# Substitution in 16x16 blocks by columns in place of rows, in a gated DeltaNet layer

## The chip, the cores and the metric

The kernel runs on one core of a Trainium2 chip. The metric is the device time of one execution in microseconds, of which the median of several runs is taken. The profile shows one further execution, instruction by instruction, on five engines: TensorE (PE; its weight loads are PEld), VectorE (DVE), ScalarE (ACT), GpSimd (POOL) and SyncE (SP), which issues most DMAs.

## What the reference computes

One layer of a hybrid backbone over 2048 latent tokens and 256 context tokens, 1024 wide: an adaLN-modulated input, a projection to 10272 columns, a bidirectional gated DeltaNet with 8 heads of 128 (branch A), a gated short convolution (branch B), a merge, an output projection and a LayerNorm. What the change touches is the inverse of a unit triangular matrix in each chunk of branch A:

```python
m = jnp.where(tri_strict, jnp.einsum('bhncd,bhnsd->bhncs', k_beta, k) * decay, 0.0)
eye = jnp.eye(CHUNK, dtype=jnp.float32)
t_inv = lax.linalg.triangular_solve(eye + m, jnp.broadcast_to(eye, m.shape), left_side=True, lower=True)
u = jnp.einsum('bhncs,bhnsv->bhncv', t_inv, v_beta)
...
v_new = u_i - jnp.einsum('bhck,bhkv->bhcv', w_i, s)
o = jnp.einsum('bhck,bhkv->bhcv', q_dec_i, s) + jnp.einsum('bhcs,bhsv->bhcv', qk_i, v_new)
s = s * d_i[..., None, None] + jnp.einsum('bhck,bhcv->bhkv', k_dec_i, v_new)
```

## The kernel before

The program has three parts. First come the projections (`projections`, `strassen`), which leave q, k, v, gates and decays in HBM. Then comes a window (`window`), in which 36 visits (18 chunks of 128 tokens in two directions, d = 0 and d = 1, in turn) carry the state, while the dense products of branch B and of the output of branch A ("fillers", L1249 to L1253) fill TensorE between the visits' own products. Last comes `final`, the output projection.

A visit inverts a 128x128 unit triangular matrix for each of 8 heads, by doubling: blocks of 16, then 32, 64 and 128. Its steps are spread over four turns of a loop, in which v0 to v3 are four successive visits. In one turn the loop writes, in this order: the state's product for v0 (`st_ks`, L300, and its sum on VectorE, L302), the loads of v3 (`visit_load`, among them gcb, the decays of all heads, L104), the first product of the 32-blocks for v1 (`inv_w16`, L210), the QK product for v2 (`gram`, L158, and its product with the decays on VectorE, L167, a piece for each head), the second one for v1 (`inv_d16`, L222, with L224 and L226 on VectorE, which write r32 and its transpose r32t), the decays of v3 (`visit_decay`, L128 to L142), the values, outputs and state sums of v0 (`st_v` L309, `st_o` L320 and L321, `st_u` L328 and L333 on VectorE) with the 64-blocks (`inv_w32`, L247, reads r32t) and 128-blocks (`inv_w64`, L278, reads r64t) of v1 between them, and at the end N for v3 (`gram`, L158 and L167) and its 16-blocks (`inv_base`). What `inv_base` makes for a visit is read one whole turn later, by `inv_w16`.

In 20 of the 36 visits, those of the four context chunks and the first to reach a latent chunk, N is formed in this way; 16 of them are latent and form QK so too. In the other 16 both come from HBM, kept by the visit in the other direction, and are multiplied by the decays in one piece each (L152).

TensorE runs in the order in which the loop is written. The instructions of every other engine are put in order by a planner when the program is built: among those whose inputs it takes to be ready it goes by the order in which they are written, and each engine then runs its list in that order.

`inv_base` takes the diagonal 32-blocks of -N by ACT (L177), folds the 16-blocks of each into 16 columns (n16: L180 on ACT, L181 and L182 on VectorE), and solves for R, the inverses of all 16x16 blocks, with 16 rows of each block in 16 partitions, and 8 heads of 16 columns in each partition. R begins as the identity (L185, GpSimd). The substitution goes row by row: row i of R is spread over the 16 partitions of its block (a shuffle, L191), multiplied by column i of n16 (L192) and added to R (L193). Each of the three reads what the one before has written. Then ACT spreads R into r32 (L196) and VectorE transposes it into r32t (L198).

Of the kernel before, what the change touches and what calls it, by code (L numbers as in the profile page):

```python
# [7 lines left out]
F32 = mybir.dt.float32  # L8
FR = mybir.dt.float32r
AF = mybir.ActivationFunctionType  # L10
ALU = mybir.AluOpType
# [4 lines left out]
P = 128  # L16
D = 1024
KT = 8
H = 8
# [13 lines left out]
def bc(ap, n):  # L33

    return ap.to_broadcast([ap.shape[0], ap.shape[1], n])


class Kern:
# [132 lines left out]
    def inv_base(self, v):  # L171
        nc, g2, d, N = self.nc, self.g2, v["d"], v["N"]

        v["n32"] = n32 = g2.tile([P, H, 32], F32, name="n32")
        for g in range(4):
            s = slice(32 * g, 32 * g + 32)
            nc.scalar.mul(out=n32[s], in_=N[s, :, s], mul=-1.0)  # L177
        n16 = g2.tile([P, H, 16], F32, name="n16")
        rows = lambda t: t.unsqueeze(1).to_broadcast([P, H, 16])
        nc.scalar.mul(out=n16, in_=n32[:, :, 0:16], mul=self.m16[0])  # L180
        nc.vector.scalar_tensor_tensor(out=n16, in0=n32[:, :, 16:32], scalar=self.m16[1], in1=n16, op0=ALU.mult, op1=ALU.add)  # L181
        nc.vector.tensor_tensor(out=n16, in0=n16, in1=rows(self.tri16[d]), op=ALU.mult)  # L182

        R = g2.tile([P, H, 16], F32, name="R16")
        nc.gpsimd.tensor_copy(out=R, in_=rows(self.i16))  # L185
        rb = g2.tile([P, H, 16], F32, name="rb")
        for i in (range(15, 0, -1) if d == 0 else range(0, 15)):
            c0, c1 = (i, 16) if d == 0 else (0, i + 1)
            w = c1 - c0
            rbv = rb.rearrange("p h c -> p (h c)")[:, 0:H * w].rearrange("p (h c) -> p h c", c=w)  # L190
            nc.vector.stream_shuffle(rbv, R[:, :, c0:c1], [i] * 16 + [16 + i] * 16)  # L191
            nc.vector.tensor_tensor(out=rbv, in0=rbv, in1=bc(n16[:, :, i:i + 1], w), op=ALU.mult)  # L192
            nc.vector.tensor_tensor(out=R[:, :, c0:c1], in0=R[:, :, c0:c1], in1=rbv, op=ALU.add)  # L193
        v["r32"] = r32 = g2.tile([P, H, 32], F32, name="r32")
        for hf in range(2):
            nc.scalar.mul(out=r32[:, :, 16 * hf:16 * hf + 16], in_=R, mul=self.m16[hf])  # L196
        v["r32t"] = r32t = g2.tile([P, H, 32], F32, name="r32t")
        nc.vector.transpose(self.fl(r32t), self.fl(r32))  # L198
# [1447 lines left out]
```

## Time and profile before

| what | value |
|---|---|
| median of 3 runs | 3217.88 us (3211.53 to 3222.15) |
| the profiled execution | 3213.67 us |
| its span, first to last instruction | 3211.9 us |
| PE busy | 2935.4 us (91%) |
| DVE busy | 2222.2 us (69%) |
| ACT busy | 1512.2 us (47%) |
| POOL busy | 1467.2 us (46%) |
| mean granted TensorE clock | 0.965 |

Busy time is the time in which an engine has at least one instruction in work; instructions of one engine may overlap at their ends. The shares are over the whole span, while the substitution runs from 1840 to 2836 us alone. The chain of waits goes back from the last instruction to what released it, step by step; what lies on it set the end.

### The profile page before, as it was taken

How to read it: one execution, taken by the hardware profiler on the slowest of the kernel's cores; microseconds unless marked ns; L12 is line 12 of the kernel's file. 1: busy time of each engine (PE TensorE's matmuls, PEld its weight loads, DVE VectorE, ACT ScalarE, POOL GpSimd, SP SyncE). 2: the span in 40 equal slices, each digit the busy share in tenths (PEclk: the TensorE clock that was granted, in tenths of full speed). 3: DMA queues.
4: the chain of work that ended last, by engine and by line, in shares of the span. 5: the costliest groups of instructions: out<-in, count | busy, mean ns of one | idle time of the engine just before them, and what ended most of it. 6: DMA issues, size and time to landing. Idle time of an engine off the chain costs nothing.

```text
span 3211.9 us, 60563 instructions
## 1 busy us (share of the span) xinstructions
PE 2935.4 (91%) x22089; PEld 2411.4 (75%) x22089; DVE 2222.2 (69%) x5843; ACT 1512.2 (47%) x3405; POOL 1467.2 (46%) x1080
## 2 busy tenths in 40 slices
PE   7899899999998999999999988898999889896997
PEld 4678668888887777788878767788887777784776
DVE  7756746566656575566652268999999988866399
ACT  4564554333445646333344335555656656652121
POOL 3543547766567555566656402333322132315264
PEclk9999999999999999999999989999999889998999
DMA  5533773323565433222233387667677777787742
GB/s 211 143 110 90 231 221 112 102 79 122 175 195 173 126 89 97 58 88 79 79 124 109 117 283 253 218 235 254 212 264 272 261 237 264 247 268 248 238 152 102
DMA packets 405384, 557.26 MB, mean 173 GB/s; under 512 B 28245, under 2 KB 278614, under 8 KB 404061
## 3 DMA queue, kind: packets, MB, share of 16 engines
q1 hardware_dynamic: 395982, 545.94, 52.6%
q10 hardware_dynamic: 9102, 7.45, 0.7%
q8 instruction: 173, 2.83, 0.4%
q14 instruction: 127, 1.03, 0.1%
HBM read 391.66 MB, written 161.64 MB: 172 GB/s over the span
## 4 chain that ended last, share of the span: by engine, by line
PE 47%; DVE 26%; issue 7%; DMA 6%; ACT 6%; POOL 4%; SPq 1%; DVEq 0%; ACTq 0%; POOLq 0%
PE pd L763 12%; PE pd L764 12%; PE pd L765 12%; DVE R L193 3%; DVE rb L192 3%; POOL al L347 2%; DVE gcb L140 2%; DVE rb L191 2%; DVE t L1008 1%; DMA gcb<-gcd 1%; POOL s L749 1%; PE pf L1253 1%; ACT n L177 1%; PE pf L1249 1%; DVE t L1010 1%
## 5 line engine op out<-in xcount | busy, mean ns | idle before, releaser
L763 PE MATMUL pd<-bh,ah 128*128 128x512 f32 x2240 | 890.5, 398 | 10.4 <-ACT u L783 5.8
L765 PE MATMUL pd<-bh,al 128*128 128x512 f32 x2240 | 877.7, 392 | 0.0
L764 PE MATMUL pd<-bl,ah 128*128 128x512 f32 x2240 | 877.0, 392 | 0.0
L347 POOL TENSOR_TENSOR al<-s,ah 128x512 fp32r<-128x512 f32 x348 | 478.9, 1380 | 471.9 <-ACT ah L346 459.9
L347 POOL TENSOR_TENSOR al<-raw,ah 128x512 fp32r<-128x512 f32 x260 | 372.0, 1435 | 321.7 <-ACT ah L346 296.0
L763 PEld LDWEIGHTS pd<-bh,ah 128*128 128x128 f32 x2240 | 423.9, 189 | 98.9 <-issue 6.6
L765 PEld LDWEIGHTS pd<-bh,al 128*128 128x128 f32 x2240 | 423.4, 189 | 90.7 <-POOL al L347 0.4
L764 PEld LDWEIGHTS pd<-bl,ah 128*128 128x128 f32 x2240 | 424.3, 189 | 85.4
L346 ACT CAST ah<-s 128x512 fp32r<-128x512 f32 x352 | 214.6, 618 | 299.7 <-PE pd L764 265.8
L346 ACT CAST ah<-raw 128x512 fp32r<-128x512 f32 x264 | 162.4, 616 | 263.5 <-PE pd L764 166.7
L749 DVE TENSOR_TENSOR s<-s,raw 128x512 f32<-128x512 f32 x80 | 107.1, 1338 | 220.5 <-POOL s L749 216.3
L1249 PE MATMUL pf<-ah,wh 128*128 128x512 f32 x512 | 213.0, 417 | 43.1 <-DMA wh<-w_ahd 20.9
L1253 PE MATMUL pf<-ah,wl 128*128 128x512 f32 x512 | 219.3, 429 | 5.1 <-DMA wl<-w_ald 5.1
L1251 PE MATMUL pf<-al,wh 128*128 128x512 f32 x512 | 213.1, 416 | 2.1 <-POOL al L347 1.3
L138 POOL TENSOR_TENSOR qd<-qd,qT 128x1024 f32<-128x1024 f32 x32 | 76.5, 2391 | 256.9 <-ACT qd L137 242.4
L192 DVE TENSOR_TENSOR rb<-rb,n 128x8 f32<-128x8 f32 (+6 forms) x540 | 170.2, 316 | 4.8
L193 DVE TENSOR_TENSOR R<-R,rb 128x8 f32<-128x8 f32 (+6 forms) x540 | 157.4, 293 | 6.0
L1249 PEld LDWEIGHTS pf<-ah,wh 128*128 128x128 f32 x512 | 101.5, 198 | 65.8 <-issue 32.6
L118 POOL TENSOR_TENSOR kt<-kt,kd 128x1024 f32<-128x1024 f32 x36 | 70.2, 1950 | 154.7 <-DMA kt<-kd 108.9
L1025 ACT ACTIVATE t<-t 128x512 f32<-128x512 f32 (+1 forms) x112 | 67.2, 600 | 144.4 <-DVE t L1010 144.3
L140 DVE SCALAR_TENSOR_TENSOR gcb<-gcb,gc,mask 128x128 f32<-128x128 f32 x288 | 127.6, 449 | 4.8 <-ACT qd L137 2.7
L1253 PEld LDWEIGHTS pf<-ah,wl 128*128 128x128 f32 x512 | 101.2, 198 | 29.8 <-DMA wl<-w_ald 9.1
(353 smaller groups left out, 5982.1 us busy)
## 6 DMA issues: line engine op xcount, KB each, us to landing
raw<-in_w_in SPq DMA_DIRECT2D x160, 512.0 KB
kT<-kTd SPq DMA_DIRECT2D x36, 512.0 KB
gcb<-gcd SPq DMA_DIRECT2D x36, 512.0 KB
kt<-kd SPq DMA_DIRECT2D x36, 512.0 KB
vh<-vd SPq DMA_DIRECT2D x36, 512.0 KB
wh<-w_bhd SPq DMA_DIRECT2D x32, 512.0 KB
wl<-w_bld SPq DMA_DIRECT2D x32, 512.0 KB
qT<-qTd SPq DMA_DIRECT2D x32, 512.0 KB
```

Source lines behind the costliest of these rows:

```text
L140: nc.vector.scalar_tensor_tensor(out=gcb[:, h, :], in0=gcb[:, h, :], scalar=gcT[:, h:h + 1], in1=self.mask[d], op0=ALU.subtract, op1=ALU.min)
L192: nc.vector.tensor_tensor(out=rbv, in0=rbv, in1=bc(n16[:, :, i:i + 1], w), op=ALU.mult)
L193: nc.vector.tensor_tensor(out=R[:, :, c0:c1], in0=R[:, :, c0:c1], in1=rbv, op=ALU.add)
L346: self.nc.scalar.copy(out=hi, in_=src)
L347: (eng or self.nc.gpsimd).tensor_tensor(out=lo, in0=src, in1=hi.bitcast(F32), op=ALU.subtract)
L749: eng.tensor_tensor(out=o, in0=a, in1=b, op=op)
L763: mm(ps, hi[:, k, :], bh, start=(first and k == 0), stop=False, skip_group_check=not first)
L764: mm(ps, hi[:, k, :], bl, start=False, stop=False, skip_group_check=not first)
L765: mm(ps, lo[:, k, :], bh, start=False, stop=(last and k == 3), skip_group_check=not first)
L1249: mm(ps, wh[:, k, :], ah, start=(k == 0), stop=False)
L1251: mm(ps, wh[:, k, :], al, start=False, stop=False)
L1253: mm(ps, wl[:, k, :], ah, start=False, stop=(k == KT - 1))
```

## The change

The substitution goes by columns. Before, R is built from rows of R itself: each step spreads a row of R that the step before has completed. After, R = I - R N is solved column by column: each step spreads row j of n16, which is there from the start, multiplies it by column j of R, which the step before has completed, and adds it to the columns still to be finished. The spread row goes into one of three buffers instead of one, and the shuffle of the next step is written between this step's product and sum. Direction d = 0 takes j from 0 to 14 and d = 1 from 15 to 1, with 15 columns left at first and one at last; before, the number of columns rose from 1 to 15.

```diff
         R = g2.tile([P, H, 16], F32, name="R16")
         nc.gpsimd.tensor_copy(out=R, in_=rows(self.i16))
-        rb = g2.tile([P, H, 16], F32, name="rb")
-        for i in (range(15, 0, -1) if d == 0 else range(0, 15)):
-            c0, c1 = (i, 16) if d == 0 else (0, i + 1)
-            w = c1 - c0
-            rbv = rb.rearrange("p h c -> p (h c)")[:, 0:H * w].rearrange("p (h c) -> p h c", c=w)
-            nc.vector.stream_shuffle(rbv, R[:, :, c0:c1], [i] * 16 + [16 + i] * 16)
-            nc.vector.tensor_tensor(out=rbv, in0=rbv, in1=bc(n16[:, :, i:i + 1], w), op=ALU.mult)
-            nc.vector.tensor_tensor(out=R[:, :, c0:c1], in0=R[:, :, c0:c1], in1=rbv, op=ALU.add)
+        order = list(range(0, 15) if d == 0 else range(15, 0, -1))
+        left = lambda j: slice(j + 1, 16) if d == 0 else slice(0, j)
+
+        def row(j):
+            c = left(j)
+            w = c.stop - c.start
+            t = g2.tile([P, H * 15], F32, name="rb", bufs=3)[:, 0:H * w].rearrange("p (h c) -> p h c", c=w)
+            nc.vector.stream_shuffle(t, n16[:, :, c], [j] * 16 + [16 + j] * 16)
+            return t
+
+        nxt = row(order[0])
+        for i, j in enumerate(order):
+            t, c = nxt, left(j)
+            nc.vector.tensor_tensor(out=t, in0=t, in1=bc(R[:, :, j:j + 1], c.stop - c.start), op=ALU.mult)
+            if i < 14:
+                nxt = row(order[i + 1])
+            nc.vector.tensor_tensor(out=R[:, :, c], in0=R[:, :, c], in1=t, op=ALU.add)
         v["r32"] = r32 = g2.tile([P, H, 32], F32, name="r32")
```

## Rows read from the trace of the kernel before

**Rows 1.** Busy sums by stretch: stretch, its us, busy (instructions) PE, PEld, DVE, ACT, POOL
```profile
1867.00:2331.00 464.00, 419.75 (x6240) 370.64 (x6240) 416.46 (x1862) 258.67 (x550) 132.69 (x107) 0.97 0.70 240
2331.00:2837.00 506.00, 441.11 (x6425) 382.31 (x6425) 455.76 (x1934) 309.98 (x834) 126.84 (x86) 0.93 0.75 259
```
**Rows 2.** Chain of waits by line, from 1867 to 2331 us, then 2331 to 2837
```profile
by line: DVE R L193 12.2%; DVE rb L192 10.9%; DVE rb L191 8.5%; DMA gcb<-gcd 6.4%; DVE N L167 6.0%; DVE QK L167 6.0%; DVE gcb L140 5.9%; issue 4.2%; ACT n L177 3.9%; DVE S L333 3.0%; PE gram L158 2.7%; DVE vh L302 2.0%; DVE gt L1192 1.9%; D
...
by line: DVE gcb L140 7.1%; DVE rb L192 5.9%; DVE R L193 5.8%; issue 5.1%; DVE rb L191 4.6%; PE pf L1253 3.5%; PE pf L1251 3.4%; PE pf L1249 3.3%; PE pst L309 3.2%; ACT n L177 3.1%; DVE N L152 2.6%; DVE S L333 2.5%; DMA gcb<-gcd 2.3%; DVE v
```
**Rows 3.** Groups of instructions: form, count, busy us, mean ns, idle before
```profile
L192 DVE TENSOR_TENSOR rb<-rb,n 128x8 f32<-128x8 f32 (+6 forms) x540 | 170.2, 316 | 4.8
L193 DVE TENSOR_TENSOR R<-R,rb 128x8 f32<-128x8 f32 (+6 forms) x540 | 157.4, 293 | 6.0
...
L191 DVE STREAM_SHUFFLE rb<-R 128x72 f32<-128x72 f32 (+7 forms) x540 | 118.8, 222 | 0.0
```
**Rows 4.** DVE timeline: start us, us, line, operation; links alone; first, middle, last
```profile
1870.75 0.17 DVE L192 TENSOR_TENSOR rb<-rb,n 128x8 f32<-128x8 f32 x1
1870.95 0.17 DVE L193 TENSOR_TENSOR R<-R,rb 128x8 f32<-128x8 f32 x1
...
2102.83 0.22 DVE L191 STREAM_SHUFFLE rb<-R 128x64 f32<-128x64 f32 x1
2103.09 0.23 DVE L192 TENSOR_TENSOR rb<-rb,n 128x64 f32<-128x64 f32 x1
2103.35 0.22 DVE L193 TENSOR_TENSOR R<-R,rb 128x64 f32<-128x64 f32 x1
...
2103.61 0.23 DVE L191 STREAM_SHUFFLE rb<-R 128x72 f32<-128x72 f32 x1
...
2835.47 0.28 DVE L192 TENSOR_TENSOR rb<-rb,n 128x120 f32<-128x120 f32 x1
2835.79 0.29 DVE L193 TENSOR_TENSOR R<-R,rb 128x120 f32<-128x120 f32 x1
```
**Rows 5.** DVE timeline where other work stands between the links
```profile
2098.37 0.34 DVE L167 SCALAR_TENSOR_TENSOR QK<-gram,cc,gcb 128x128 f32<-128x128 f32 x1
2098.63 0.17 DVE L192 TENSOR_TENSOR rb<-rb,n 128x24 f32<-128x24 f32 x1
2098.72 0.34 DVE L167 SCALAR_TENSOR_TENSOR QK<-gram,cc,gcb 128x128 f32<-128x128 f32 x1
```
**Rows 6.** Chain of waits in order of time: start us, us, what
```profile
2128.95 0.02 issue
2128.97 0.22 DVE R L193
```
**Rows 7.** DVE timeline: the first shuffle and the first product of one visit
```profile
2119.23 0.16 DVE L191 STREAM_SHUFFLE rb<-R 128x8 f32<-128x8 f32 x1
...
2122.48 0.87 DVE L192 TENSOR_TENSOR rb<-rb,n 128x8 f32<-128x8 f32 x1
```
**Rows 8.** DVE timeline: the transpose that the 64-blocks read, in two visits
```profile
2100.53 0.44 DVE L226 STREAM_TRANSPOSE r32t<-r 128x256 f32<-128x256 f32 x1
...
2127.68 0.44 DVE L226 STREAM_TRANSPOSE r32t<-r 128x256 f32<-128x256 f32 x1
```
**Rows 9.** PE timeline in the same two visits; idle before it in brackets
```profile
2102.13 0.69 PE L247 MATMUL pinv<-r32t,N 32*32 32x32 f32 x32
...
2128.18 0.69 PE L247 MATMUL pinv<-r32t,N 32*32 32x32 f32 x32
2129.91 0.49 PE L320 MATMUL pst<-S,qd 128*128 128x128 f32 x2 [1.03 <-ACT ot L1287]
...
2136.00 1.14 PE L278 MATMUL pinv<-r64t,N 64*64 64x64 f32 x16 [1.64 <-ACT r64t L267]
```
**Rows 10.** SyncE's waits (us, times, longest), 1867 to 2331; a load on the chain
```profile
SPq L104 <- DVE QK L167: 27.0, 13, 2.6
...
2100.20 5.76 DMA gcb<-gcd
```

## The prediction

> **What bounds the kernel now.** The change lies in one function, which runs only in the windowed part of the program, so I first read the busy sums by stretch [rows 1]. From 1867 to 2331 us VectorE is busy 416 of 464 us, and from 2331 to 2837 us 456 of 506. TensorE is busy 420 and 441 us. What the reader should see is that both engines are nearly full, so busy shares alone don't say which one a saving must reach. The chain of waits over the same two stretches does [rows 2]. In the first, the three lines of the substitution (L191 shuffle, L192 product, L193 sum) are 31.6% of it, and nothing of TensorE's comes near. In the second they are 16.3%, with TensorE's dense products, its state products and ACT mixed in. So the first stretch goes at VectorE's pace, and the second partly does.
>
> Then the groups of these lines [rows 3]: 540 of each, 15 in each of 36 visits, 170, 157 and 119 us busy. The timeline shows two ways in which they run. Alone, each waits for the one in front of it, since the shuffle reads the row that the sum has just written, the product reads the shuffled row, and the sum reads the product [rows 4]: a product of 0.23 us starts at 2103.09, the sum at 2103.35, the next shuffle at 2103.61. A start comes 0.03 to 0.04 us after the end of the one before. With other work in between [rows 5], a product of 0.17 us starts at 2098.63 and the next, independent, instruction at 2098.72, 0.08 us before its end. A dependent neighbour therefore costs 0.035 + 0.08 = 0.12 us that an independent one doesn't.
>
> I counted such dependent neighbours among the three lines in VectorE's timeline: 479, of which [rows 4] show the first pair, a middle run and the last pair; 281 of them stand in the first stretch and 198 in the second. At 0.12 us they are 57 us of empty VectorE time. Not all of it matters: where the chain of waits passes through the pair, as in [rows 6], the gap is on the path. That holds for 211 of the 281 and 78 of the 198, together 289, or 35 us. The others lie beside a load or beside TensorE's work.
>
> **The change part by part.** *Instructions.* Fifteen shuffles, products and sums a visit as before, and the widths are the same set, one to fifteen columns of eight heads, only from wide to narrow. Products and sums take the same forms, with the broadcast operand from R instead of n16. I cost this at nothing; it would matter only if a form ran differently, and then against the 446 us of [rows 3], for which no row speaks.
>
> *The order of waits.* A step now has one pair of neighbours that must wait, a sum and the next product, which needs the column just finished. Product and shuffle are independent. Shuffle and sum are too, and the sum's own input, the product, is one instruction further back: with the intervals of [rows 4] and [rows 5] the product is ready 0.23 + 0.035 = 0.26 us after its start, and the sum's turn comes after 0.15 + 0.15 = 0.30 us, so it waits for nothing. At narrow widths (0.17 us long, 0.09 apart) 0.18 stands against 0.20, a miss of 0.02 that I leave out. So two of three gaps go: 289 x 2/3 x 0.12 = 23 us on the path. Bounds: nothing, if the gap belongs to the engine and not to the wait; 35 us, if the planner also puts a later shuffle between sum and product (three buffers allow one ahead); 57 us, if also the gaps off the path turn out to hold VectorE up. I take 23, because the lines as written give just this and [rows 6] show what the path is made of.
>
> Between a dependent and an independent neighbour lie 0.12 us [rows 4, 5]. A page of the Trainium skill speaks against the change here: "VectorE: DVE Perf Modes", section "The DRAIN you can't avoid", says that a pipeline flush follows every operation in any case, and that eight copies took the same time with a semaphore after each as with one after the last. By that the term would be 0, in place of 23; this trace disagrees with it by the 0.12 us.
>
> *The first shuffle.* Before, it reads R, which is ready early, and it runs well ahead of the first product: 2119.23 against 2122.48 [rows 7]. Now it needs n16 and stands right before that product. That is 0.08 (0.16 less the overlap) to 0.20 us (with the wait) in a visit, 3 to 7 us in 36; below that 0, where the visit isn't on VectorE's path. I take 3.
>
> *The buffers.* A row buffer was last read by a sum of an earlier step on the same engine, more than one interval back, so I cost this at nothing; a wait in each step would be 0.12 us x 14 x 36 = 60 us, and only a planner that lets the buffers run dry would bring it.
>
> Sum: -23 + 3 = -20 us. Against the profiled execution's 3213.67 us (span 3211.9, with 1.8 us around it) that is 3193.7. The median of the runs lies 4.2 us above that execution, so for a median I say 3198. What can be told from no change is about 0.3%, 9.7 us.
>
> **The rivals.** *More goes than the path shows* (3160 to 3186 us). When VectorE gets faster, what waited for it moves too. For it: in [rows 1] VectorE is busy 90% of both stretches, and the chain of waits is only one of several nearly equal paths. Against it: TensorE's 420 of 464 us leaves 44 us in the first stretch at most. All 57 us gone gives 3160.
>
> *The gap stays whatever stands between* (3221 us). Then only the 3 us of the first shuffle are left. Against it [rows 4, 5]: the same line starts its successor 0.04 us after or 0.08 before its end, according to who the successor is. It is what the page's section on the flush, named above, would make of this kernel.
>
> *The gain is given back to a load* (3211 us). The decay factors gcb are loaded only when the last QK product (L167) has been taken, and the load lasts 5.76 us [rows 10]; 13 times that product ended the wait. The substitution has fewer gaps to fill this time with, and if the QK products end 1 us later because more links stand among them, 13 us come back: -20 + 13 = -7. Against it: pairs beside that load are not among my 289.
>
> *Slower: the substitution pushes the inverse's next level back* (3236 us). In [rows 5] one link alternates with one QK product, so a link goes first whenever it is ready; a link that waits lets one other through. After the change only one link in three waits, and three links go for one other. Eight QK products and the two operations of the next level (L224, L226) stand in that stretch in each of the 16 visits that form QK by heads, so L226 ends 20 links later than now, 20 x 0.09 to 0.15 = 1.8 to 3 us, less what the substitution has already got through. TensorE comes to the product that needs it (L247) at 2128.18, when L226 has ended at 2127.68 + 0.44 = 2128.12; in another visit at 2102.13 against 2100.97 [rows 8, 9]. So it has 0.06 to 1.2 us to spare and would wait the rest. Against it: later in the same visit TensorE waits 1.03 and 1.64 us for ACT [rows 9], which a later arrival would swallow, and VectorE has the links behind it by then, so that the decays and state sums run without any between them. It cancels the gain at a net wait of 20/16 = 1.25 us a visit and makes the kernel slower by 0.3% at 1.9; at 2.4 us it gives 38 - 20 = +18, 3236, and at the full 3 us 3246.
>
> **How the numbers follow.** The forecast, with its own range from 3186 to 3208, gets 0.50: the gap is measured and the path goes through it, but how the planner mixes the links with the rest is not in this trace. More than that 0.13, the gap stays 0.04, given back 0.15, slower 0.18. Faster by over 0.3% is then 0.63, within it 0.19, slower 0.18. The range runs from all gaps gone (3160) to the edge of the slower case (3228), which leaves that case's 0.18 out.
>
> **What would show it.** Right: L191 to L193 still 540 each; shuffles that start before their product has ended; dependent neighbours down from 479 to under 200, nearly all of them a sum and a product; the windowed part about 20 us shorter, and the other two parts unchanged. The substitution would end earlier in each visit, and its share of the chain of waits would fall below a quarter in the first stretch. Wrong: sums that still start after their product's end plus 0.035 us with a shuffle between; VectorE idle before L128 or before the N products of L167; TensorE waiting at L247 for r32t of L226 by a microsecond or more in each visit, with a lower granted clock behind it. The last is the one that would turn the sign.

## The result, and the profile after

The changed kernel takes 3247.09 us (median of 4 runs, 3243.44 to 3255.24), the kernel before on the same chip 3220.02 (4 runs). The ratio is 1.0090, with a 95% interval of 1.0069 to 1.0111: slower by 0.9%, 27 us by the medians. The profiled execution took 3243.44 us with a span of 3241.7, 29.8 longer than that of before. The forecast was 3198, with a range of 3160 to 3228.

Nearly all of the loss lies in the windowed part. Before 1830 us nothing has moved. The first stretch begins and ends at the same place in the work as that of [rows 1]; the second one's end, 2870 us, lies some 5 us further on in the work than 2837 does there. The busy sums of the changed kernel, in the columns of [rows 1]:

```profile
1867.00:2358.00 491.00, 431.21 (x6220) 383.02 (x6219) 392.81 (x1863) 262.53 (x549) 135.46 (x109) 0.93 0.67 225
2358.00:2870.00 512.00, 444.96 (x6574) 382.12 (x6574) 433.08 (x1938) 311.69 (x839) 125.78 (x85) 0.94 0.77 262
```

Against [rows 1] the first stretch is 27 us longer, with nearly the same instructions. The last visit's products with R (L309, now L318) end 28 us later than before (2893.89 against 2865.77), so the second stretch adds 1 or 2 us to the 27, and what comes behind the visits another 2. VectorE is busy 24 us *less* in the first and 23 in the second, so the engine that the change was to relieve is relieved: its share falls from 90% to 80% of the first stretch. The granted clock of that stretch falls from 0.97 to 0.93. A saving on VectorE has come out as idle time.

The groups of the three lines, shuffle (L193 now), product (L199) and sum (L202), to be set beside [rows 3]:

```profile
L199 DVE TENSOR_TENSOR rb<-rb,R 128x120 f32<-128x120 f32 (+4 forms) x540 | 140.2, 260 | 2.9 <-DVE rb L193 0.3
L202 DVE TENSOR_TENSOR R<-R,rb 128x120 f32<-128x120 f32 (+4 forms) x540 | 134.7, 250 | 1.1
...
L193 DVE STREAM_SHUFFLE rb<-n 128x120 f32<-128x120 f32 (+4 forms) x540 | 117.0, 222 | 0.1
```

There are 540 of each, as forecast, and the products and sums are shorter by 53 us together. The same lines on the chain of waits, first stretch, then second ([rows 2] before):

```profile
by line: DVE rb L193 8.5%; DVE R L202 7.0%; DVE rb L199 6.4%; DVE N L167 6.2%; DVE QK L167 5.9%; PE pf L1262 5.2%; ACT n L177 4.4%; PE pinv L287 3.9%; PE gram L158 3.8%; DVE vh L311 3.5%; PE pf L1258 3.4%; PE pf L1260 3.4%; PE pinv L297 3.3
...
by line: DVE gcb L140 8.8%; DVE rb L193 6.1%; DVE R L202 4.8%; DVE rb L199 4.5%; issue 4.4%; DVE vh L311 4.4%; PE pf L1262 3.3%; PE pf L1258 3.3%; PE pf L1260 3.2%; ACT n L177 3.1%; ACT jk L1406 3.0%; PE pst L309 2.9%; PE pinv L297 2.4%; AC
```

The three lines have gone from 31.6% to 21.9% of the first stretch; what has come in their place is TensorE (dense products L1258 to L1262, the 128-blocks' L287). Who made TensorE late is said by its waits in the first stretch (line, what for: us in total, times, longest), here the first four of five rows:

```profile
PE pinv L256 <- DVE r32t L235: 38.3, 14, 5.8
PE pinv L287 <- ACT r64t L276: 6.6, 8, 0.9
PE pinv L231 <- ACT w L222: 5.3, 3, 2.3
PE pst L318 <- DVE vh L311: 4.9, 4, 2.2
```

The same view of the kernel before, in its first stretch:

```profile
PE pinv L222 <- ACT w L213: 11.0, 11, 2.3
PE pinv L278 <- ACT r64t L267: 8.9, 12, 1.6
PE pst L320 <- ACT ot L1287: 7.7, 8, 1.0
...
PE pinv L247 <- DVE r32t L226: 2.9, 4, 1.3
```

And VectorE's own waits in the changed kernel, the same columns:

```profile
DVE N L167 <- ACT zat L163: 23.2, 12, 4.0
DVE gt L1201 <- PE pf L1262: 18.6, 6, 6.6
DVE t L128 <- DMA gcb<-gcd: 13.0, 11, 1.6
DVE vh L311 <- PE pst L309: 11.9, 12, 1.0
```

L256 and L235 are L247 and L226 of the kernel before, the pair of [rows 8, 9]. Before, TensorE waited 2.9 us in 4 visits; now it waits 38.3 in 14 (and 7.6 more in 3 of the second stretch). VectorE waits afterwards, for what TensorE now delivers late. One visit in VectorE's timeline (start us, us) shows how it comes about. The links (shuffles, products and sums) stand as the change wrote them, and the other work stands among them:

```profile
2078.03 0.24 DVE L199 TENSOR_TENSOR rb<-rb,R 128x96 f32<-128x96 f32 x1
...
2078.21 0.24 DVE L193 STREAM_SHUFFLE rb<-n 128x80 f32<-128x80 f32 x1
2078.36 0.24 DVE L202 TENSOR_TENSOR R<-R,rb 128x96 f32<-128x96 f32 x1
2078.52 0.34 DVE L167 SCALAR_TENSOR_TENSOR QK<-gram,cc,gcb 128x128 f32<-128x128 f32 x1
2078.78 0.23 DVE L199 TENSOR_TENSOR rb<-rb,R 128x88 f32<-128x88 f32 x1
...
2082.39 0.34 DVE L167 SCALAR_TENSOR_TENSOR QK<-gram,cc,gcb 128x128 f32<-128x128 f32 x1
...
2082.76 0.35 DVE L233 SCALAR_TENSOR_TENSOR r<-pinv,m16h,r 128x128 f32<-128x128 f32 x1
...
2083.23 0.44 DVE L235 STREAM_TRANSPOSE r32t<-r 128x256 f32<-128x256 f32 x1
```

and TensorE in the same visit, with its idle time in brackets:

```profile
2080.08 0.39 PE L330 MATMUL pst<-v,QK 128*128 128x128 f32 x2
2080.30 1.06 PE L337 MATMUL pst<-v,kt 128*128 128x128 f32 x8
2083.72 1.06 PE L256 MATMUL pinv<-r32t,N 32*32 32x32 f32 x32 [2.36 <-DVE r32t L235]
2084.71 0.80 PE L329 MATMUL pst<-S,qd 128*128 128x128 f32 x2
2085.30 0.64 PE L330 MATMUL pst<-v,QK 128*128 128x128 f32 x2
```

A product, a shuffle and a sum go, then one QK product, then the next three. Only the product has to wait for its neighbour, so only one place in three is open to other work; in [rows 5] each second one was. Eight QK products, L233 and L235 take 5.9 us to get through (2077.77 to 2083.67). TensorE has nothing else to do from 2081.36 on, and starts L256 0.05 us after L235's end. After it, the pairs of products that had taken 0.39 us take 0.64: from 2070 to 2081 the granted clock is 1.00 (2.4 GHz), from 2084.6 to 2088.4 it is 0.50 (1.2 GHz), with the idle time between. VectorE, which has the links behind it at 2086.2, then stands 1.4, 2.3, 1.1 and 3.2 us before 2099.4.

### The profile page after: what moved, and what is told of

It reads as the page before. It is cut to its first block, busy times and chain, and to the rows that moved or that the text cites. A ratio compares the mean times of both kernels' runs of the same rounds, so it can differ in the third digit from the quotient of the medians.

```text
span 3241.7 us, 60662 instructions
## 1 busy us (share of the span) xinstructions
PE 2948.6 (91%) x22089; PEld 2422.8 (75%) x22089; DVE 2169.8 (67%) x5843; ACT 1517.7 (47%) x3405; POOL 1468.3 (45%) x1080
## 4 chain that ended last, share of the span: by engine, by line
PE 49%; DVE 23%; ACT 7%; issue 7%; DMA 5%; POOL 4%; SPq 1%; DVEq 0%; ACTq 0%; POOLq 0%
PE pd L772 11%; PE pd L773 11%; PE pd L774 11%; POOL al L356 2%; DVE rb L193 2%; DVE R L202 2%; DVE gcb L140 2%; DVE rb L199 2%; PE pf L1262 2%; DVE t L1017 1%; PE pf L1258 1%; POOL s L758 1%; DVE vh L311 1%; PE pf L1260 1%; ACT n L177 1%
## 5 line engine op out<-in xcount | busy, mean ns | idle before, releaser
L1258 PE MATMUL pf<-ah,wh 128*128 128x512 f32 x512 | 214.3, 420 | 40.4 <-DMA wh<-w_ahd 17.3
L1262 PE MATMUL pf<-ah,wl 128*128 128x512 f32 x512 | 221.1, 433 | 2.8 <-DMA wl<-w_ald 2.7
L1258 PEld LDWEIGHTS pf<-ah,wh 128*128 128x128 f32 x512 | 102.6, 200 | 62.3 <-issue 24.6
L140 DVE SCALAR_TENSOR_TENSOR gcb<-gcb,gc,mask 128x128 f32<-128x128 f32 x288 | 135.4, 525 | 17.6 <-ACT qd L137 16.4
L199 DVE TENSOR_TENSOR rb<-rb,R 128x120 f32<-128x120 f32 (+4 forms) x540 | 140.2, 260 | 2.9 <-DVE rb L193 0.3
L202 DVE TENSOR_TENSOR R<-R,rb 128x120 f32<-128x120 f32 (+4 forms) x540 | 134.7, 250 | 1.1
L1262 PEld LDWEIGHTS pf<-ah,wl 128*128 128x128 f32 x512 | 101.9, 199 | 27.6 <-DMA wl<-w_ald 6.3
```

What stands on the lines that cost most here:

```text
L140: nc.vector.scalar_tensor_tensor(out=gcb[:, h, :], in0=gcb[:, h, :], scalar=gcT[:, h:h + 1], in1=self.mask[d], op0=ALU.subtract, op1=ALU.min)
L199: nc.vector.tensor_tensor(out=t, in0=t, in1=bc(R[:, :, j:j + 1], c.stop - c.start), op=ALU.mult)
L202: nc.vector.tensor_tensor(out=R[:, :, c], in0=R[:, :, c], in1=t, op=ALU.add)
L1258: mm(ps, wh[:, k, :], ah, start=(k == 0), stop=False)
L1262: mm(ps, wl[:, k, :], ah, start=False, stop=(k == KT - 1))
```

## The experiments

All are timed against the kernel before on the same chip; the ratios are of the time to that of the kernel before. My theory: the links hardly wait any more, and so go nearly in one piece ahead of what was written behind them; the step from 16- to 32-blocks of the visit ahead (`inv_d16`, now L233 and L235, here called level 16) comes late, TensorE stands, and that outweighs the gaps saved. The rivals: the new formula is slower by itself (A), the QK products end late and so gcb is freed late (B, D), and others named below.

**Level 16 ahead.** In `inv_d16`, where `high_priority(200)` moves instructions forward in the planner's order:

```diff
-        nc.vector.scalar_tensor_tensor(out=r32[:, :, cs], in0=dp[:, :, cs], ...)
-        nc.vector.transpose(self.fl(r32t), self.fl(r32))
+        with self.tc.high_priority(200):
+            nc.vector.scalar_tensor_tensor(out=r32[:, :, cs], in0=dp[:, :, cs], ...)
+            nc.vector.transpose(self.fl(r32t), self.fl(r32))
```

> The changed kernel, and the two VectorE instructions that end level 16 (the product into r32, L233, and its transpose, L235) stand ahead of the substitution in VectorE's queue: five or six links stand before them where twenty did, and the QK products come behind them. Theory (the substitution goes first and makes L235 some 4 us late, TensorE stands at L256 and its clock falls): the wait of TensorE for r32t at L256, 38.3 us in the stretch of the first visits and 7.6 in the second, falls under 8 in both together, the granted clock of the first stretch comes back from 0.93 to 0.96 or more, and the time is 3195 to 3215. Rival A (the new formula itself, by columns from wide to narrow, or its buffers, is slower): 3235 to 3250 with L256's wait gone or not. Rival B (the QK products' end, which frees gcb for its next load, is what is late): 3240 or more, since QK now ends later still, with VectorE's wait for gcb over the 13.0 us of the changed kernel.

Measured: 3215.06 us, ratio 0.9995 (0.9974 to 1.0016), at the upper edge of the theory's 3195 to 3215. The wait at L256 is gone (no row of it is left), the clock of the first stretch is 0.96, and the time is that of the kernel before: 0.95%, or 31 us, have come back. Rivals A and B fall, since the formula is untouched and the QK products end 0.8 us later in a visit than in the changed kernel. But nothing was gained over the kernel before, and TensorE's waits from 1850 to 2850 us name the next one:

```profile
PE pst L319 <- DVE vh L312: 23.2, 28, 3.1
```

L312 (L311 in the changed kernel) are the eight products into vh, ready just when the links begin. `st_v` (L319) needs them.

**The substitution written later.** The loop becomes a function of its own, `inv_sub`, called in the next turn behind level 16:

```diff
                 if v1:
                     self.inv_d16(v1)
+                if v2:
+                    self.inv_sub(v2)
                 if v3:
                     self.visit_decay(v3)
```

> The changed kernel, with the substitution (from R = I to the transpose into r32t) written in the next turn, behind level 16 of the visit ahead of it: in VectorE's queue all eight QK products and L233 and L235 then stand before all but the first link, and the loop starts when they are done. Theory: TensorE's wait at L256 falls under 8 us in both stretches, the granted clock of the first stretch is 0.96 or more, and since the dependent neighbours stay few (about 110 where the kernel before has 479) the time is below both kernels, 3185 to 3208. Rival A (the formula): 3235 to 3250. Rival C (the substitution, begun later, ends too late for level 16 of its own visit): TensorE waits over 15 us for r32t at the first products of that level, and the time is 3225 or more.

Measured: 3190.62 us, ratio 0.9915 (0.9886 to 0.9944), inside the theory's 3185 to 3208. No wait at the first products of the next level (`inv_w32`, L256 of the changed kernel), and 1.3 us for the substitution's own r32t. Rivals A and C fall.

**The kernel before with the same move.**

> The kernel before with the same move of its substitution (by rows, with its gaps) behind level 16 of the visit ahead. Theory: the kernel before loses only 2.9 us at that place, because other work fits between its links, so the move brings little, 3205 to 3222; the difference from the changed kernel with the same move is the price of the gaps on the chain, 10 to 25 us. Rival A (the formula by columns is slower by itself): this kernel is faster than the changed one with the same move by 20 us or more.

Measured: 3221.98 us, ratio 1.0023 (1.0006 to 1.0040). So by rows the moved kernel is 0.2% slower than the kernel before, and by columns 0.85% faster; between the two lie 31 us, over the 10 to 25 expected. The reason stands in its waits: with the gaps in it the substitution, begun later, comes to its end too late for the first product of its own level 16 (L215 is L210 of before; the wait there was 7.8 us in 6):

```profile
PE pinv L215 <- DVE r32t L203: 23.7, 18, 3.5
```

**By columns, each shuffle in line.** The formula of the change without its issue order:

```diff
-        nxt = row(order[0])
         for i, j in enumerate(order):
-            t, c = nxt, left(j)
+            t, c = row(j), left(j)
             nc.vector.tensor_tensor(out=t, in0=t, in1=bc(R[:, :, j:j + 1], c.stop - c.start), op=ALU.mult)
-            if i < 14:
-                nxt = row(order[i + 1])
```

with one buffer for the spread row.

> The changed kernel's formula by columns, with one buffer for the spread row and each shuffle issued right before its product, as the kernel before has it: each link waits for the one before, and other work stands among the links again. Theory: L235 comes in time as in the kernel before, TensorE's wait at L256 is under 10 us in both stretches, dependent neighbours are over 400, and the time is that of the kernel before, 3205 to 3225. Rival A (the formula itself is what costs): 3235 to 3250, with the wait at L256 small.

Measured: 3217.90 us, ratio 1.0008 (0.9992 to 1.0024), with 499 dependent neighbours and 5.7 us of wait at the place of L256. VectorE is busy 2221.8 us, as in the kernel before. In this order, columns in place of rows are worth nothing and cost nothing. What made the changed kernel slow is its issue order; the three buffers that go with it were kept in the runs above, which are not slow.

**Level 16 and vh ahead.** As the first run, with the eight products into vh (`st_ks`) under the same `high_priority(200)`.

> The run with level 16 ahead, and the eight products into vh (L311, issued on VectorE right before) ahead of the substitution as well; the QK products stay among the links, one to three of them. Theory: in the run with level 16 ahead the same delay went to the next work behind the links, and TensorE stood 23.2 us at L319 for vh; with vh ahead that wait falls under 6 us and the time is 3185 to 3205. Rival D (what holds that run at the time of the kernel before is that its QK products end late and gcb is freed late): the wait for vh goes and the time stays at 3208 to 3222, with VectorE idle over 60 us in its waits for gcb, qd and the filler's products.

Measured: 3194.69 us, ratio 0.9935 (0.9917 to 0.9952). No wait for vh and none for r32t is left on TensorE. That is 0.60%, 19 us, for vh's place alone. The time lies inside the theory's 3185 to 3205, and outside the 3208 to 3222 of rival D. VectorE's waits for gcb and the fillers' products are still 21.5 and 19.5 us in this run; of the first, 16.4 are one wait (16.8 in the kernel before).

**Level 16 and QK ahead, vh not.** The QK products under the same priority in place of vh.

> The run with level 16 ahead, and the eight QK products ahead of the substitution as well; vh stays behind four links as in the changed kernel. Theory: TensorE's wait for vh stays at 12 to 25 us, and the time is 3198 to 3215, above the run with vh ahead. Rival D (the QK products' end): 3185 to 3200, below the run with vh ahead.

Measured: 3248.48 us, ratio 1.0104 (1.0082 to 1.0126). Both expectations miss, the theory by 33 us. Its direction holds, since this is the slower of the two runs, and VectorE's timeline shows how far it went:

```profile
2063.33 0.34 DVE L313 SCALAR_TENSOR_TENSOR vh<-pst,ngam,vh 128x128 f32<-128x128 f32 x1
2063.59 2.15 DVE L168 SCALAR_TENSOR_TENSOR QK<-gram,cc,gcb 128x128 f32<-128x128 f32 x8
2065.66 0.34 DVE L235 SCALAR_TENSOR_TENSOR r<-pinv,m16h,r 128x128 f32<-128x128 f32 x1
...
2067.30 0.34 DVE L313 SCALAR_TENSOR_TENSOR vh<-pst,ngam,vh 128x128 f32<-128x128 f32 x1
```

The eighth vh product now stands behind all that was put ahead. TensorE waits for vh 36 times, 21.8 us together. That is a third of the 68 us by which this run lies above the next, which differs in vh's place alone; the rest shows as further waits behind `st_v` (r64t 29.5 us in 23, VectorE before N 42.9 in 14 and for gcb 43.4 in 16), which I did not take apart. The clock has no part in it: it is 0.98 from 1867 to 2348 us, and that stretch is 40 us longer than the like one of the run with level 16 and vh ahead.

**Vh, QK and level 16 ahead.** All three under `high_priority(200)`; the substitution stays where the change wrote it.

> The changed kernel with vh, the QK products and level 16 all ahead of the substitution by priority, its text left where it is: VectorE's queue is then nearly that of the kernel with the substitution moved to the next turn. Theory (the order in VectorE's queue is all that the move changed): the time of that run within 0.4%, 3180 to 3203. Rival E (the move gained by the buffers R16, r32 and r32t being taken later, and not by the order): 3205 or more.

Measured: 3180.22 us, ratio 0.9889 (0.9871 to 0.9907). With vh ahead already, the place of the QK products is thus worth another 0.46%, or 14 us, where without vh ahead it cost 1.1%. Why is open: in the profiled executions the first stretch, in which most of these products stand, takes the same time with them ahead or not (440.5 and 440.6 us from the first piece of n32, L177, to the first of the 19th visit), and the difference lies behind it.

Beside it the moved substitution ran once more:

> The changed kernel with the substitution written in the next turn, once more on this chip for its interval against the kernel before: 0.9885 to 0.994 of it if the earlier run told the truth (3183 to 3200), over 0.996 if that was luck of five runs.

Measured: 3187.36 us, ratio 0.9918 (0.9899 to 0.9937). The two are 0.2 to 0.3% apart, and rival E falls. VectorE's timeline with all three ahead:

```profile
2087.71 2.16 DVE L314 SCALAR_TENSOR_TENSOR vh<-pst,ngam,vh 128x128 f32<-128x128 f32 x8 [0.80 <-PE pst L311]
...
2091.03 2.16 DVE L168 SCALAR_TENSOR_TENSOR QK<-gram,cc,gcb 128x128 f32<-128x128 f32 x8 [0.26 <-ACT zat L163]
2093.11 0.34 DVE L235 SCALAR_TENSOR_TENSOR r<-pinv,m16l,r 128x128 f32<-128x128 f32 x1
2093.37 0.27 DVE L200 TENSOR_TENSOR rb<-rb,R 128x120 f32<-128x120 f32 x1
```

and its busy sums in the two stretches, to be set beside [rows 1]:

```profile
1867.00:2312.00 445.00, 420.78 (x6270) 373.43 (x6269) 385.73 (x1880) 261.47 (x554) 133.99 (x109) 0.97 0.74 251
2312.00:2809.00 497.00, 440.75 (x6419) 377.29 (x6419) 440.79 (x1928) 308.79 (x830) 125.81 (x84) 0.93 0.78 264
```

With what TensorE waits for out of the way, the first stretch is 19 us shorter between the cuts than before the change (25 from the first piece of n32 to that of the 19th visit), and TensorE is busy 95% of it.

**The kernel before with the same three ahead, and the best version again.**

> The kernel before (by rows, with its gaps), with vh, the QK products and level 16 ahead of the substitution by the same priorities. Theory: its chain of links is longer by the gaps (0.12 us at each of 44 neighbours, up to 5 us of a visit) and with nothing early to fill them it now ends at TensorE's heels: TensorE waits over 15 us for the r32t of the substitution, and the time is 3208 to 3235; the changed formula under the same order (3180) is then 0.9 to 1.7% faster, which is what the two gaps per link are worth once nothing is held up. Rival F (the order alone gives the gain, the formula nothing): 3175 to 3195.

> The changed kernel with vh, the QK products and level 16 ahead, once more for its interval beside the run above: 3172 to 3190, ratio to the kernel before 0.987 to 0.992.

Measured: 3261.48 us, ratio 1.0143 (1.0126 to 1.0160), by rows, and 3177.96, ratio 0.9882 (0.9864 to 0.9900), by columns. Rival F falls: the order that gains 1.2% by columns costs 1.4% by rows. The waits show why, and the loss is larger than the 3208 to 3235 us expected: the links, with their gaps and started last, end too late for TensorE's next product of theirs (L211, once L210):

```profile
PE pinv L211 <- DVE r32t L199: 49.2, 18, 5.9
```

The runs side by side. The times in a visit are medians over 16 visits (the 7th to the 22nd) of the profiled executions, read from the timeline: from the first vh product's start to the last one's end; from the start of n32 (L177) to the end of level 16's transpose (L226); from the substitution's first product to its last sum; and the mean period of a visit.

| kernel | ratio | vh, us | to L226's end, us | substitution, us | period, us |
|---|---|---|---|---|---|
| before | 1 | 3.35 | 8.79 | 19.2 | 26.4 |
| changed | 1.0090 | 4.94 | 12.85 | 11.8 | 28.2 |
| level 16 ahead | 0.9995 | 5.36 | 7.66 | 14.9 | 26.3 |
| level 16 and vh ahead | 0.9935 | 2.16 | 7.48 | 14.6 | 25.3 |
| level 16 and QK ahead | 1.0104 | 7.44 | 7.33 | 13.3 | 28.1 |
| vh, QK, level 16 ahead | 0.9889 | 2.16 | 6.75 | 13.4 | 24.9 |
| substitution later | 0.9915 | 3.62 | 7.32 | 14.8 | 25.4 |
| before, substitution later | 1.0023 | 3.36 | 7.51 | 21.8 | 27.2 |
| before, vh, QK, level 16 ahead | 1.0143 | 2.55 | 5.47 | 21.3 | 29.1 |
| columns in line | 1.0008 | 3.79 | 9.20 | 19.6 | 26.1 |

The substitution is shortest of all in the changed kernel. Its period is nevertheless the longest of those by columns, with vh and level 16 late; where neither is, the shorter substitution comes through.

## Why the prediction was wrong, point by point

*Instructions, costed at nothing: right in effect, not in busy time.* The kernel by columns in line has the time of the kernel before. VectorE's busy time fell by 52 us in the changed kernel all the same, for a reason given at the end.

*The order of waits, -23 us: right in its count, and not a gain in this place.* Dependent neighbours among the three lines fell from 479 to 111, those on the chain of waits from 289 to 30, at the same 0.12 us each: 31 us off the path, 8 more than the two thirds that I took. Shuffle and sum stand without a gap 339 times, as worked out. With the other work in order the formula by columns is 31 us faster than that by rows (substitution later, against the kernel before with the same move). In the version by rows TensorE waits 23.7 us for r32t, so this pair doesn't size the gaps by themselves; the versions by columns with vh, QK and level 16 ahead are 27 to 40 us faster than the kernel before, but by the order and the gaps together. The size of the term is thus not shown by itself.

In the changed kernel's timeline the 339 sums behind a shuffle start 0.09 us before its end, and the 111 dependent neighbours start 0.03 us after. The Trainium skill, page "VectorE: DVE Perf Modes", section "The DRAIN you can't avoid", reports that a semaphore after each of eight copies cost nothing extra, though it adds that a next operation that is not held starts earlier. For these short operations the trace shows a price of a wait, 0.12 us.

*The first shuffle (+3) and the buffers (0)* are too small to be told apart.

*The step that failed is the one that put the saving on the path with nothing lost behind it.* I took a gap for lost time. In [rows 5] it was the place through which vh, QK and level 16 got ahead of a chain that the planner lets go first; to close the gaps is to move that work back. I saw this and worked it out as the slower rival, at 38 us less the gain, with a chance of 0.18 and outside my range. What decided is shown by the runs: L235 ends 4.1 us later in a visit (12.85 against 8.79), where I had 1.8 to 3, and TensorE waits 45.9 us in 17 visits, 2.7 each. The count of 20 links was right (in 14 of the 16 visits of the table 34 stand before L235 now, and 14 stood before L226); a link's price was too low, 0.2 us in place of 0.09 to 0.15. The wide links now go first (0.24 us long in the visit above, 0.17 in [rows 5]), which may be why. To put level 16 ahead gives back 31 us, near the 38. The second part I left out altogether: the eight products into vh stand in front of QK in the same place, finish 1.6 us later, and are worth another 19 us. Against these 50 us stand the 23 of the forecast: 3218 + 50 - 23 = 3245, and measured were 3247. That this closes so well is in part luck: it stops at vh, and the 14 us that QK's place brings besides stand in none of its terms.

*What I set against that rival held in part.* TensorE's other waits in the first stretch, most of them for ACT, fell from 40.4 to 21.1 us, so that 19 of the 35 us more at L256 did not lengthen its idle time. But TensorE's clock fell behind the wait, so the products after it took longer, and VectorE, done with the links, found nothing to do until TensorE delivered. By the busy sums TensorE's idle time in the stretch grew by 16 us and its busy time by 11, for nearly the same products at a mean clock of 0.93 in place of 0.97. How much of the loss is the clock was not separated further; the run with QK ahead lost as much at a clock of 0.98 in the first stretch.

*Given back to the load of gcb.* VectorE waits 13.0 us for it in the first stretch, where it waited 1.9 before. But with level 16 ahead the QK products end 0.8 us later still (12.7 against 11.9 us after n32 starts, median), and no wait for gcb is left in that stretch. So this wait follows from the stall and isn't its cause.

## What to carry to other kernels

A gap in a dependent chain on a busy engine is not empty where a planner fills it: before closing it, list what goes through it and by when each piece is needed on the other engines. A chain that no longer waits acts as one block, and its place in the queue then matters more than its length: here the same columns are 0.9% slower where they stand ahead of vh, QK and level 16, and 1.2% faster behind them. So change the place together with the chain, and test both alone: by rows the new place costs 0.2 to 1.4%, and by columns the old one costs 0.9%.

## What the runs showed of the hardware that was not expected

VectorE's products and sums of two tensors sometimes take several times as long. In the kernel before, 85 of the substitution's 1080 take over 0.45 us, 111 us together or 1.3 each, where the others take 0.22 on average; in the changed kernel it is 47, 53 us together. Over the usual 0.22 us that is 93 us before and 43 after, and the difference of 50 is about as much as VectorE's busy time fell (52). Each of the 85 and of the 47 overlaps an operation of two tensors on GpSimd and ends with it, to 0.15 us. In the kernel before, GpSimd's timeline and VectorE's beside it:

```profile
2122.28 2.04 POOL L164 TENSOR_TENSOR zat<-zat,cc 128x512 f32<-128x512 f32 x2 [3.40 <-ACT zat L163]
```

```profile
2123.27 0.34 DVE L302 SCALAR_TENSOR_TENSOR vh<-pst,ngam,vh 128x128 f32<-128x128 f32 x1
2123.53 0.81 DVE L193 TENSOR_TENSOR R<-R,rb 128x8 f32<-128x8 f32 x1
```

GpSimd is through at 2124.32 and the sum at 2124.34, while the vh product, which reads one of its tensors from PSUM, takes its usual 0.34 us in between. The Trainium skill, page "Trainium Architecture — The Big Picture", section "What this means for kernel authors", says that VectorE and GpSimd share a port pair under an exclusive lock and no other engines contend on that side; the rows agree for two-tensor operations. It matters for readings like mine: a mean duration from the groups ([rows 3]: 316 ns) holds such waits, and where the links stand changes it.
